# Down-projections: two of four weight sums of a seven-product chunk by transfers, and a third seven-product chunk in the first halves

## The chip, the cores and the metric

The kernel runs on one core of a Trainium2 chip. The metric is device time in microseconds, the median of several runs; lower is better. Engines are named as the profile names them: PE (matrix products) with its weight loads PEld, DVE (VectorE), ACT (ScalarE), POOL (GpSimd), SP (SyncE, which here only issues loads).

## What is computed

Two layers over 256 positions of width 2048, in float32. Each layer is a token mixer and then a gated feed-forward part, and the change lies in the last product of the latter:

```python
def conv_ffn(h, w_up, conv_w, conv_b, w_down):
    u = h @ w_up                          # 2048 -> 11264
    u = conv_width_3(u) + conv_b          # along positions, per channel
    gate, val = jnp.split(u, 2, axis=-1)  # 5632 each
    return (jax.nn.silu(gate) * val) @ w_down   # 5632 -> 2048
...
h = h + conv_ffn(rms_norm(h, ffn_norm[i]), w_up[i], conv_w[i], conv_b[i], w_down[i])
```

## The kernel before

**Tiles.** `w_down` is 11 chunks of 512 rows by four column blocks of 512. A *load* brings half of a chunk's column block, 128 partitions by 1024 numbers, 512 KB, into one of six `raw` buffers (`NRAW`; line 137, issued by SP, which takes its orders one after the other). A float32 factor is split into a high part in float32r and the rest: ACT copies `raw` to `wh` (line 129), DVE subtracts to get `wl` (line 130), and a product is three matmuls, high by high, low by high, high by low. Four pairs `wh`/`wl` go round (`NHL` and one more in the down-projections).

**Stages.** `ffn` works in two halves (`HALVES`), chunks 0 to 5 and 6 to 10. In each half the up-projections make the chunks' activations, and then the down-projection takes the column blocks in pairs, (0,1) and (2,3), each pair by `project_pair`. In layer 0's second half, blocks 2 and 3 are plain projections; in layer 1's second half the pair (2,3) is the `tail`.

**Passes.** `project_pair` goes through a list of passes (`units`), which `weave` writes out. A *column pass* ("c", chunk, i) loads one buffer, splits it and makes 12 matmuls. A *product pass* ("P", chunk, p) is one of the seven products that replace the eight block products of a chunk and a pair of column blocks (Winograd's form); it makes 6 matmuls. So a plain chunk costs a pair 4 x 12 = 48 matmuls, and a seven-product chunk 7 x 6 = 42, with 7 splits in place of 4. `SKG` says which chunks of each half go by seven products: 0 and 2 in both; the tail takes the first alone.

**Weight sums.** The chunk's four weight blocks are "11", "12", "21", "22". Products 1, 2 and 3 take blocks 11, 21 and 22 as loaded, the others take sums, which DVE makes in place in `raw` (line 251) one pass ahead, in `prepare`:

```python
        sums = {5: ("11", "12"), 7: ("12", "22"), 6: ("22", "11"), 4: ("21", "22")}
```

The order of the products is `ORDER` = 1, 2, 5, 3, 7, 6, 4. In a first half each product pass is followed by one column pass while there are any (in pair (0,1) not behind the first product of a chunk, `lone`), after four column passes ahead for the pair (0,1) and one for (2,3).

**Activation sums.** A seven-product chunk needs seven combinations of its activations (`forms`), made and split by `glu_forms` while the next chunk is projected up; a plain chunk needs four splits (`glu`). `make_forms` does the same for chunk 0 of the next up-projection during the first half's down-projection, with its scratch in the tiles "t" and "tT". `combine` adds the products up into `h`.

**Order of the work.** Each engine has one instruction stream, whose order the framework's scheduler sets at build time from the order of the program, with splits and sums moved ahead (`AHEAD`). A `raw` buffer is handed on in the order of release; the next load into it waits until its last reader has finished.

Of the kernel before, what the change touches and what calls it, by code (L numbers as in the profile page):

```python
# [8 lines left out]
F32 = mybir.dt.float32  # L9
# [14 lines left out]
NRAW, NHL = 6, 3  # L24
SKG = ((0, 2), (0, 2))
ORDER = (1, 2, 5, 3, 7, 6, 4)
PLACE = "pava"
AHEAD = 45
# [6 lines left out]
def tile_encoder(ctx: ExitStack, tc: tile.TileContext, x, xT, w_a, w_ao, q_gain, k_gain, w_b, w_bo,  # L35
# [15 lines left out]
    nc.gpsimd.memset(nhalf, -0.5)  # L51
    ones = cpool.tile([P, P], F32, name="ones")
    nc.gpsimd.memset(ones, 1.0)
    nc.scalar.dma_start(gain, gains)
# [6 lines left out]
    def nm(s):  # L61
        uid[0] += 1
        return f"{s}_{uid[0]}"
# [152 lines left out]
    def project_pair(w, n0, n1, lhs, forms, units, late, early_done, n0_done, product_done=None, tail=False,  # L216
                     lazy=False):
        home = {1: "M1", 2: "C11", 3: "C12", 4: "C21", 5: "M5", 6: "M6", 7: "M7"}
# [22 lines left out]
        def block(kg, b):  # L241
            if (kg, b) not in blocks:
                blocks[kg, b] = load_raw(w, (n0, n1)[int(b[1]) - 1], kg, int(b[0]) - 1)
            return blocks[kg, b]

        def prepare(u):
            kind, kg, p = u
            if kind == "P" and p in sums:
                dst, src = (block(kg, b) for b in sums[p])
                with tc.high_priority(offset=AHEAD):  # L250
                    nc.vector.tensor_tensor(dst, dst, src, ALU.add)  # L251
                if p == 6:
                    done_raw(blocks.pop((kg, "11")))
                elif p == 4:
                    done_raw(blocks.pop((kg, "22")))

        last_s = max(i for i, u in enumerate(units) if u[0] == "P")
        for i, (kind, kg, p) in enumerate(units):
# [4 lines left out]
            else:  # L263
                b = {1: "11", 2: "21", 3: "22", 5: "11", 7: "12", 6: "22", 4: "21"}[p]
                r = block(kg, b)
            if i + 1 < len(units):
                prepare(units[i + 1])
            wh, wl = split_raw(r, kind == "c" or p in (7, 4))
            if kind == "P" and p in (7, 4):
                blocks.pop((kg, b))  # L270
# [281 lines left out]
    def ffn(l, hT, ss_in, g_next, last, side=None):  # L552
        with tc.tile_pool(name=nm("wpool"), bufs=1) as wp, tc.tile_pool(name=nm("fpool"), bufs=1) as fp:
# [5 lines left out]
            fin = []  # L559
            cr = fp.tile([P, 3, P], F32, name=nm("cr"))  # L560
            rows = conv[l].rearrange("b o (r c) -> (b o r) c", c=P)
# [13 lines left out]

            us = [fp.tile([P, 1040], F32, name=nm("u"))[:, :1032].rearrange("p (j c) -> p j c", j=4) for _ in range(2)]
            for u in us:
                nc.gpsimd.memset(u[:, :, P:P + 1], 0.0)

# [40 lines left out]
            def form_tiles():  # L620
                xs, ts = (fp.tile([P, 4, NT], F32, tag=t, name=nm("xs")) for t in ("t", "tT"))
                return xs, ts, [fp.tile([P, 2, NT], F32R, tag=t, name=nm("fm"), bufs=3) for t in ("cg", "cg", "cv", "cv")]

            def glu_forms(cg, cv, fm, hh):
# [34 lines left out]
            for hf, (p0, p1) in enumerate(HALVES):  # L659
# [3 lines left out]
                def new_form():  # L663
                    pool, k = next(tags)
                    return tuple(pool.tile([P, NT], F32R, tag=f"a{c}{k}", name=nm("a" + c)) for c in "hl")

                wide.append(1)
                for p in range(p0, p1):
                    if p - p0 in SKG[hf]:
                        fm = forms[p - p0] = {f: new_form() for f in (1, 7, 2, 5, 4, 6, 3) + (0,) * hf}  # L670
                        if hf:
                            for kt in range(4):
                                slots[4 * (p - p0) + kt] = [
                                    tuple(t[:, kt % 2 * P:(kt % 2 + 1) * P] for t in fm[f])
                                    for f in ((1, 0), (2, 4))[kt // 2]]
                    else:
                        slots.update({4 * (p - p0) + j: new_form() for j in range(4)})
# [92 lines left out]
                def weave(lead, late, tail):  # L770
                    ks = SKG[hf][:1] if tail else SKG[hf]
                    c = [("c", k, i) for k in range(np_) if k not in ks for i in range(4)]
                    ps = [("P", k, p) for k in ks for p in ORDER]
                    if tail:
                        c0, c1 = ([u for u in c if u[2] // 2 == n] for n in range(2))
                        c = c0[:-1] + c1[:4] + c0[-1:] + c1[4:-2]
                    units = []
                    units += [c.pop(0) for _ in range(lead)]
                    lone = (ps[0], ps[7]) if late and hf == 0 else ()
                    rest = len(c)  # L780
                    for i, u in enumerate(ps):
                        n = min(1, len(c))
                        if late and hf == 1:
                            n = (i + 1) * rest // len(ps) - i * rest // len(ps)
                        units += [u] + [c.pop(0) for _ in range(n) if u not in lone]
                    return units + c
# [12 lines left out]
                def pair(n0, n1, late, tail=False):  # L799
# [3 lines left out]
                                       lambda a: start(combine(a, n0, n1, fp, "s", combined)),  # L803
                                       lambda a: first_half(a, n0, n1), tail=tail)
                    accs = acc["C12"], acc["C22"]
# [7 lines left out]
                if hf == 0:  # L813
                    start(make_forms(first_forms, hT, 0, form_tiles))
                if hf == 0 or last:
# [564 lines left out]
```

## Time and profile before

| | |
|---|---|
| time, median of 3 runs | 2236.48 us (2235.53 to 2237.12) |
| span of the profiled execution | 2235.3 us; what lies around it is some 1.2 us, taken against the median |
| PE busy | 2222.8 us (99%), 10021 matmuls |
| DVE, ACT, POOL busy | 1838.0 us (82%), 1549.9 us (69%), 329.7 us (15%) |
| granted clock of PE | 0.999 |
| loads of `w_down` | 176 of 512 KB, 4.9 us from issue to landing (median) |
| sums of weight blocks by DVE (line 251) | 92 of 1226 ns; 52 of them in the down-projections |

The profile is one execution. A view of windows gives the busy time of each engine in stretches of time; matmul records overlap (each has some 0.39 us, while the next starts earlier), so PE's busy time says little, and starts and counts say more. "Released by" is what ended an engine's idle time.

### The profile page before, as it was taken

What the parts mean: (1) busy time and instruction counts of PE and PEld (TensorE: products, weight loads), DVE (VectorE), ACT (ScalarE), POOL (GpSimd) and SP (SyncE); (2) the same over time, 40 slices, a digit from 0 to 9 for tenths busy, and PEclk for the clock granted to TensorE, in tenths of its full rate; (3) what the DMA queues carried; (4) which work ended last, traced back from release to release, by engine and by line L of the source; (5) the groups of instructions that cost most, each with busy time, mean ns of one, the idle gap of its engine ahead of it and who ended that gap; (6) DMA issues with size and microseconds to landing.
All of it is one profiled execution on the core that took longest, in us unless ns stands there. A gap on an engine that the chain in (4) does not pass through costs nothing.

```text
span 2235.3 us, 29163 instructions
## 1 busy us (share of the span) xinstructions
PE 2222.8 (99%) x10021; PEld 1840.0 (82%) x10021; DVE 1838.0 (82%) x2523; ACT 1549.9 (69%) x2393; POOL 329.7 (15%) x482
## 2 busy tenths in 40 slices
PE   9999999999999999999999999999999999999998
PEld 7888888888888888888888888888888888888886
DVE  6777778888888788979877978786887898888897
ACT  7665677777557777767876777576777754677764
POOL 2210212210001010011340213010110100001101
PEclk9999999999999999999999999999999999999999
DMA  8444656766556665666655565565566666556654
GB/s 303 164 145 151 206 189 208 243 202 191 199 197 201 200 192 176 225 204 205 212 178 191 166 206 179 188 198 187 193 195 192 197 198 211 190 193 192 227 183 151
DMA packets 126501, 437.44 MB, mean 196 GB/s; under 512 B 17313, under 2 KB 18081, under 8 KB 126353
## 3 DMA queue, kind: packets, MB, share of 16 engines
q1 hardware_dynamic: 119744, 425.64, 58.1%
q0 software_dynamic: 6176, 9.39, 1.7%
q8 instruction: 78, 1.28, 0.2%
q14 instruction: 71, 0.57, 0.1%
q10 hardware_dynamic: 432, 0.56, 0.1%
HBM read 429.20 MB, written 6.29 MB: 195 GB/s over the span
## 4 chain that ended last, share of the span: by engine, by line
PE 93%; DVE 3%; issue 1%; DMA 1%; POOL 1%; ACT 1%; SPq 0%; DVEq 0%; POOLq 0%; ACTq 0%
PE acc L155 18%; PE acc L156 18%; PE acc L154 18%; PE acc L286 11%; PE acc L291 11%; PE acc L288 11%; DVE wl L130 2%; DMA raw<-in_w_down_dram 1%; PE ps L291 1%; PE ps L321 1%; PE ps L286 1%; PE ps L288 1%; PE ps L325 0%; POOL pp L361 0%; PE ps L324 0%
## 5 line engine op out<-in xcount | busy, mean ns | idle before, releaser
L130 DVE TENSOR_TENSOR wl<-raw,wh 128x1024 fp32r<-128x1024 f32 x861 | 1056.8, 1234 | 266.4 <-ACT wh L129 262.3
L129 ACT ACTIVATE wh<-raw 128x1024 fp32r<-128x1024 f32 x861 | 902.6, 1057 | 467.5 <-PE acc L156 166.3
L154 PE MATMUL acc<-wh,xh 128*128 128x512 f32 x1664 | 649.2, 391 | 0.0
L155 PE MATMUL acc<-wl,xh 128*128 128x512 f32 x1664 | 648.8, 390 | 0.3 <-DVE wl L130 0.2
L156 PE MATMUL acc<-wh,xh 128*128 128x512 f32 x1664 | 648.1, 389 | 0.0
L155 PEld LDWEIGHTS acc<-wl,xh 128*128 128x128 f32 x1664 | 312.6, 188 | 67.4 <-DVE wl L130 2.8
L156 PEld LDWEIGHTS acc<-wh,xh 128*128 128x128 f32 x1664 | 312.4, 188 | 64.6
L154 PEld LDWEIGHTS acc<-wh,xh 128*128 128x128 f32 x1664 | 312.7, 188 | 63.7 <-ACT wh L165 0.3
L286 PE MATMUL acc<-wh,ah 128*128 128x512 f32 x762 | 297.0, 390 | 0.6 <-DVE h L544 0.6
L288 PE MATMUL acc<-wh,al 128*128 128x512 f32 x762 | 296.7, 389 | 0.0
L361 POOL COPY u<-t 32x256 f32<-32x256 f32 x176 | 110.5, 628 | 1003.9 <-DVE t L591 995.7
L291 PE MATMUL acc<-wl,ah 128*128 128x512 f32 x762 | 212.0, 389 | 0.4 <-DVE wl L130 0.4
L286 PEld LDWEIGHTS acc<-wh,ah 128*128 128x128 f32 x762 | 143.1, 188 | 31.2 <-DVE h L544 1.5
L291 PEld LDWEIGHTS acc<-wl,ah 128*128 128x128 f32 x762 | 143.0, 188 | 30.4 <-DVE wl L130 0.9
L288 PEld LDWEIGHTS acc<-wh,al 128*128 128x128 f32 x762 | 143.1, 188 | 29.5
L286 PE MATMUL acc<-wh,xh 128*128 128x512 f32 x416 | 162.7, 391 | 0.0
L288 PE MATMUL acc<-wh,xh 128*128 128x512 f32 x416 | 162.0, 389 | 0.0
L363 ACT ACTIVATE u<-t 32x256 f32<-32x256 f32 x352 | 147.6, 419 | 17.8 <-DVE t L591 9.9
L251 DVE TENSOR_TENSOR raw<-raw,raw 128x1024 f32<-128x1024 f32 x92 | 112.8, 1226 | 14.8 <-DMA raw<-in_w_down_dram 14.1
L291 PE MATMUL acc<-wl,xh 128*128 128x512 f32 x416 | 113.1, 390 | 0.0
L288 PEld LDWEIGHTS acc<-wh,xh 128*128 128x128 f32 x416 | 78.1, 188 | 16.0
L286 PEld LDWEIGHTS acc<-wh,xh 128*128 128x128 f32 x416 | 78.1, 188 | 16.0
(254 smaller groups left out, 2388.9 us busy)
## 6 DMA issues: line engine op xcount, KB each, us to landing
raw<-in_w_up_dram SPq DMA_DIRECT2D x352, 512.0 KB, 4.5
raw<-in_w_down_dram SPq DMA_DIRECT2D x176, 512.0 KB, 4.9
raw<-in_w_b_dram SPq DMA_DIRECT2D x144, 512.0 KB, 4.5
raw<-in_w_bo_dram SPq DMA_DIRECT2D x48, 512.0 KB, 4.4
raw<-in_w_a_dram SPq DMA_DIRECT2D x40, 512.0 KB, 4.5
raw<-in_w_ao_dram SPq DMA_DIRECT2D x32, 512.0 KB, 3.8
raw<-in_w_a_dram SPq DMA_DIRECT2D x16, 256.0 KB, 6.1
h<-in_x_dram SPq DMA_DIRECT2D x4, 512.0 KB, 8.4
```

Of the source, the lines that this page charges most:

```text
L129: nc.scalar.activation(wh, r, AF.Copy)
L130: nc.vector.tensor_tensor(wl, r, wh.bitcast(F32), ALU.subtract)
L154: nc.tensor.matmul(accs[m], xh, wh[:, j, :], start=st, stop=False)
L155: nc.tensor.matmul(accs[m], xh, wl[:, j, :], start=False, stop=False)
L156: nc.tensor.matmul(accs[m], xl, wh[:, j, :], start=False, stop=sp)
L251: nc.vector.tensor_tensor(dst, dst, src, ALU.add)
L286: nc.tensor.matmul(acc[k], xh, wh[:, j, :], start=k in fresh, stop=False)
L288: nc.tensor.matmul(acc[k], xl, wh[:, j, :], start=False, stop=False)
L291: nc.tensor.matmul(acc[k], xh, wl[:, j, :], start=False, stop=last[k] == i and j == 1)
L321: nc.tensor.matmul(o, lh[ls], rh[rs], start=start, stop=stop)
L361: nc.gpsimd.tensor_copy(dst, src)
L363: nc.scalar.activation(dst, src, AF.Copy)
```

## The change

Thirteen seven-product chunk passes per execution become seventeen: in both first halves chunk 4 goes by seven products too. In every down-projection two of the four sums of a chunk are made by accumulating transfers that POOL issues: block 22 is added onto 12 from the weights in HBM (a second read of it), and 22, by then 22+11+12, is added onto 21 within the chip's buffers. DVE makes the other two, behind the product whose block they overwrite and no longer one pass ahead. The products' order becomes 1, 2, 3, 5, 6, 7, 4, and blocks 11 and 12 are loaded together. In the first halves the column passes are spread evenly over the 21 product passes (12 column passes: 4 or 1 ahead, 8 or 11 between). The third chunk's activation sums get room in "tT" and "junk", for which `make_forms` moves its scratch to the tiles "u" (whose edges are zeroed again afterwards), the convolution's rows move to "junk", and an unused tile `ones` goes. The products of the attention's and the up-projections' chunks keep the old order and DVE's sums.

```diff
-SKG = ((0, 2), (0, 2))
+SKG = ((0, 2, 4), (0, 2))
 ORDER = (1, 2, 5, 3, 7, 6, 4)
+ORDER_D = (1, 2, 3, 5, 6, 7, 4)
...
+        def onto(kg, b, src):
+            dst = blocks[kg, b].rearrange("p a c -> p (a c)")
+            if isinstance(src, str):
+                src = blocks[kg, src].rearrange("p a c -> p (a c)")
+            nc.gpsimd.dma_start(dst, src, accum_op=ALU.add)
+
+        def add(kg, b, src):
+            with tc.high_priority(offset=AHEAD):
+                nc.vector.tensor_tensor(blocks[kg, b], blocks[kg, b], blocks[kg, src], ALU.add)
+
+        def sums_behind(kg, p):
+            if p == 1:
+                add(kg, "11", "12")
+                if 7 in by_dma:
+                    onto(kg, "12", w[n1, kg][:, 1024:])
+                else:
+                    add(kg, "12", "22")
+            elif p == 3:
+                add(kg, "22", "11")
+                if 4 in by_dma:
+                    onto(kg, "21", "22")
+            elif p == 6 and 4 not in by_dma:
+                add(kg, "21", "22")
+                done_raw(blocks.pop((kg, "22")))
...
-            if i + 1 < len(units):
-                prepare(units[i + 1])
-            wh, wl = split_raw(r, kind == "c" or p in (7, 4))
-            if kind == "P" and p in (7, 4):
+            if by_dma:
+                if kind == "P" and p == 1:
+                    block(kg, "12")
+                if i and units[i - 1][0] == "P":
+                    sums_behind(*units[i - 1][1:])
+                free = (5, 7, 4) + (6,) * (4 in by_dma)
+            else:
+                if i + 1 < len(units):
+                    prepare(units[i + 1])
+                free = (7, 4)
+            wh, wl = split_raw(r, kind == "c" or p in free)
+            if kind == "P" and p in free:
                 blocks.pop((kg, b))
...
-            us = [fp.tile([P, 1040], F32, name=nm("u"))[:, :1032].rearrange("p (j c) -> p j c", j=4) for _ in range(2)]
-            for u in us:
-                nc.gpsimd.memset(u[:, :, P:P + 1], 0.0)
+            ut = [fp.tile([P, 1040], F32, name=nm("u")) for _ in range(2)]
+            us = [t[:, :1032].rearrange("p (j c) -> p j c", j=4) for t in ut]
+            def zero_edges():
+                for u in us:
+                    nc.gpsimd.memset(u[:, :, P:P + 1], 0.0)
...
-                xs, ts = (fp.tile([P, 4, NT], F32, tag=t, name=nm("xs")) for t in ("t", "tT"))
+                xs, ts = (t[:, :1024].rearrange("p (j c) -> p j c", j=4) for t in ut)
...
+            def first_half_forms():
+                yield from make_forms(first_forms, hT, 0, form_tiles)
+                zero_edges()
...
-                        fm = forms[p - p0] = {f: new_form() for f in (1, 7, 2, 5, 4, 6, 3) + (0,) * hf}
+                        fm = forms[p - p0] = {}
+                        if p - p0 == 4:
+                            f2 = fp.tile([P, 4, NT], F32R, tag="tT", name=nm("ff"))
+                            f1 = fp.tile([P, 512], F32R, tag="junk", name=nm("ff"))
+                            fm.update({7: (f2[:, 0], f2[:, 1]), 5: (f2[:, 2], f2[:, 3]), 6: (f1[:, :NT], f1[:, NT:])})
+                        fm.update({f: new_form() for f in (1, 7, 2, 5, 4, 6, 3) + (0,) * hf if f not in fm})
...
-                    ps = [("P", k, p) for k in ks for p in ORDER]
+                    ps = [("P", k, p) for k in ks for p in ORDER_D]
...
-                    lone = (ps[0], ps[7]) if late and hf == 0 else ()
                     rest = len(c)
                     for i, u in enumerate(ps):
                         n = min(1, len(c))
-                        if late and hf == 1:
+                        if hf == 0 or late:
                             n = (i + 1) * rest // len(ps) - i * rest // len(ps)
-                        units += [u] + [c.pop(0) for _ in range(n) if u not in lone]
+                        units += [u] + [c.pop(0) for _ in range(n)]
...
-                                       lambda a: first_half(a, n0, n1), tail=tail)
+                                       lambda a: first_half(a, n0, n1), tail=tail, by_dma=(7, 4))
```

More of the change, by code (lines that the diff above doesn't have):

```diff
@@ L51, in tile_encoder @@
     nc.gpsimd.memset(nhalf, -0.5)
-    ones = cpool.tile([P, P], F32, name="ones")
-    nc.gpsimd.memset(ones, 1.0)
     nc.scalar.dma_start(gain, gains)
@@ L216, in project_pair @@
     def project_pair(w, n0, n1, lhs, forms, units, late, early_done, n0_done, product_done=None, tail=False,
-                     lazy=False):
+                     lazy=False, by_dma=()):
         home = {1: "M1", 2: "C11", 3: "C12", 4: "C21", 5: "M5", 6: "M6", 7: "M7"}
@@ L559, in ffn @@
             fin = []
-            cr = fp.tile([P, 3, P], F32, name=nm("cr"))
+            cr = fp.tile([P, 512], F32, tag="junk", name=nm("cr"))[:, :3 * P].rearrange("p (a c) -> p a c", a=3)
             rows = conv[l].rearrange("b o (r c) -> (b o r) c", c=P)
@@ L620, in form_tiles @@
             def form_tiles():
-                xs, ts = (fp.tile([P, 4, NT], F32, tag=t, name=nm("xs")) for t in ("t", "tT"))
+                xs, ts = (t[:, :1024].rearrange("p (j c) -> p j c", j=4) for t in ut)
                 return xs, ts, [fp.tile([P, 2, NT], F32R, tag=t, name=nm("fm"), bufs=3) for t in ("cg", "cg", "cv", "cv")]
+            def first_half_forms():
+                yield from make_forms(first_forms, hT, 0, form_tiles)
+                zero_edges()
             def glu_forms(cg, cv, fm, hh):
@@ L813, in ffn @@
                 if hf == 0:
-                    start(make_forms(first_forms, hT, 0, form_tiles))
+                    start(first_half_forms())
                 if hf == 0 or last:
```

## The prediction

> **What bounds the kernel now.** I read the page's busy times first, then the down-projections' stretches in the view of windows, then the timeline for the beat of PE, and last the waits of SP and ACT there and the DMA issues.
>
> ```profile
> span 2235.3 us, 29163 instructions
> ...
> PE 2222.8 (99%) x10021; PEld 1840.0 (82%) x10021; DVE 1838.0 (82%) x2523; ACT 1549.9 (69%) x2393; POOL 329.7 (15%) x482
> ...
> 526.00:651.70 125.70, 125.12 (x552) 103.26 (x551) 112.97 (x129) 70.90 (x84) 2.58 (x4) 1.00 0.60 200
> 526.00:588.60 62.60, 62.60 (x278) 51.82 (x277) 58.13 (x74) 40.78 (x54) 2.58 (x4) 1.00 0.58 192
> 869.00:920.50 51.50, 51.50 (x229) 42.62 (x228) 50.11 (x59) 35.41 (x48) 2.58 (x4) 1.00 0.57 191
> 1778.50:1904.00 125.50, 125.43 (x553) 103.54 (x552) 113.19 (x129) 71.32 (x84) 2.59 (x4) 1.00 0.61 201
> 2172.70:2221.00 48.30, 47.85 (x211) 39.33 (x210) 43.89 (x46) 23.64 (x31) 8.43 (x5) 1.00 0.47 161
> ...
> 565.46 0.39 PE L286 MATMUL acc<-wh,ah 128*128 128x512 f32 x1
> 565.69 0.39 PE L288 MATMUL acc<-wh,al 128*128 128x512 f32 x1
> 565.91 0.39 PE L286 MATMUL acc<-wh,ah 128*128 128x512 f32 x1
> ```
>
> The rows of windows are: stretch, its length, then PE, PEld, DVE, ACT and POOL busy with counts, PE's clock, DMA share, GB/s. They are, in order, layer 0's first half (both pairs), its pair (0,1), layer 0's second-half pair, layer 1's first half, and the tail. A matmul has 0.39 us, but the next starts 0.227 us after it; so 0.227 and not 0.39 is what a matmul costs, a product pass is 6 x 0.227 = 1.36 us and a column pass 2.72. The 552 matmuls of a first half's two pairs take 552 x 0.2267 = 125.1 us of the 125.7 in the first of these rows: PE stands idle for 0.6 us in layer 0, 0.4 in layer 1, 0.5 in the tail (211 x 0.2267 = 47.8 of 48.3), nothing in the second-half pair. PE bounds these stages, and DVE is close behind, 58.1 of 62.6 us in the pair (0,1).
>
> How far the splits run ahead of PE, S below, decides what a late buffer costs:
>
> ```profile
> 520.70 1.22 DVE L130 TENSOR_TENSOR wl<-raw,wh 128x1024 fp32r<-128x1024 f32 x1
> 526.02 0.39 PE L286 MATMUL acc<-wh,ah 128*128 128x512 f32 x1
> 563.90 1.22 DVE L130 TENSOR_TENSOR wl<-raw,wh 128x1024 fp32r<-128x1024 f32 x1
> 567.27 1.07 PE L291 MATMUL acc<-wl,ah 128*128 128x512 f32 x4
> ...
> ACT wh L129 <- PE acc L288: 24.7, 21, 5.1
> ACT wh L129 <- DMA raw<-in_w_down_dram: 12.1, 7, 2.8
> ...
> SPq L137 <- DVE wl L130: 85.8, 39, 7.5
> ```
>
> Counting splits and passes in order, these are the first and the twentieth of the stretch 526 to 588.6: the first column pass needs its low part 8 matmuls after 526.02, at 527.83, and has it at 521.9, S = 5.9; the twentieth needs it at 567.27 and has it at 565.1, S = 2.2. I take S = 3. The waits (total, times, longest; 526 to 651.7) say what limits S: mostly ACT waits until PE gives back a pair, which is idle time with no price; 12.1 us it waits for loads; and SP stands 85.8 of 125.7 us before a raw buffer is free. Loads go out as fast as buffers come back.
>
> **The change part by part.**
>
> *Matmuls.* Chunk 4 costs a pair 42 in place of 48, over two pairs and two layers 24 fewer: 24 x 0.2267 = 5.44 us off the engine that bounds the stage. This is the gain.
>
> *Splits and DVE's sums.* Their prices, and the stage that makes the third chunk's activation sums:
>
> ```profile
> L130 DVE TENSOR_TENSOR wl<-raw,wh 128x1024 fp32r<-128x1024 f32 x59 | 70.9, 1220 | 7.4 <-ACT wh L129 7.0
> L251 DVE TENSOR_TENSOR raw<-raw,raw 128x1024 f32<-128x1024 f32 x17 | 20.8, 1221 | 4.8 <-DMA raw<-in_w_down_dram 4.7
> L129 ACT ACTIVATE wh<-raw 128x1024 fp32r<-128x1024 f32 x60 | 62.1, 1057 | 50.6 <-PE acc L288 24.7 <-DMA raw<-in_w_down_dram 12.1 <-DVE raw L251 8.8
> L307 DVE TENSOR_TENSOR fm<-xs,fm 128x256 fp32r<-128x256 f32 x4 | 1.7, 417 | 0.0
> ...
> 460.00:510.00 50.00, 50.00 (x222) 41.38 (x222) 39.87 (x58) 37.48 (x58) 7.46 (x12) 1.00 0.64 209
> ```
>
> In a first-half pair passes go from 30 to 33 and DVE's sums from 8 to 6: DVE has one operation more, 58.13 + 1.22 = 59.35 us, in 62.6 - 1.36 = 61.2 us; ACT has 40.8 + 3 x 1.06 = 44.0. Hidden behind PE, with 1.9 us to spare on DVE where there were 4.5. Without this cover the 1.22 us is paid in each of four pairs, 4.9 us. In the second-half pairs DVE loses 4 sums of 8 (4.9 us of 50.1) and in the tail 2 of 4; PE has nothing to regain in the former and at most 0.5 us in the latter. Over all, at most 0.6 + 0.4 + 0.5 = 1.5 us of stall can be regained. I take the tail's alone, as DVE is what is relieved there: 0.5.
>
> *The third chunk's activation sums.* Seven splits for four and four more small sums: 7 x 0.42 = 2.9 us for DVE and 3 x 0.41 = 1.2 for ACT, once a layer, while chunk 5 is projected up. There DVE has 39.9 us in 50 (last row): hidden, and 2.9 us a layer if it were not. The two small memsets of edges and the moved scratch are order on POOL and DVE, at nothing; behind a memset that waits for the sums' last split, POOL's next transfer would wait too.
>
> *The order on SP.* The same 24 loads a pair; block 12 comes 1 to 3 passes sooner, so it holds its buffer longer, block 11 shorter (given back at product 5). Evenly spread, the column passes give the products less cover: between two product passes 8/21 of a column pass and not nearly one.
>
> *The transfers.* Two of 512 KB a chunk, 34 in all, from POOL, which waits for DVE's sum before it issues; behind it stand only the last up-projection's four copies, the edges, and in the tail the final gains, none of which PE waits for soon. The trace has no accumulating transfer. The nearest rows, of windows about 2101, 1055, 367, 1130 and, for the loads beside nothing else, 526 to 588.6:
>
> ```profile
> q1 hardware_dynamic: 3291, 11.99, 57.9%
> raw<-in_w_down_dram SPq DMA_DIRECT2D x23, 512.0 KB, 4.9
> DMA to landing us min/median/max: 3.7/4.9/6.9
> ...
> btg<-scr POOLq DMA_DIRECT2D x1, 256.0 KB, 5.6
> fin<-in_final_norm_dram POOLq DMA_DIRECT2D x4, 256.0 KB, 5.1
> scr<-lnt POOLq DMA_DIRECT2D x6, 256.0 KB, 12.5
> ...
> raw<-in_w_b_dram SPq DMA_DIRECT2D x4, 512.0 KB, 4.3
> raw<-in_w_down_dram SPq DMA_DIRECT2D x5, 512.0 KB, 5.9
> raw<-in_w_b_dram SPq DMA_DIRECT2D x4, 512.0 KB, 7.4
> bt<-scr POOLq DMA_DIRECT2D x3, 256.0 KB, 7.2
> ```
>
> From below it is the fastest load, 3.7 us; from above, POOL's transfers out in small pieces, 12.5. Between: 57.9% of 62.6 us for 11.99 MB is 3.0 us of all 16 engines per MB, so 1.6 us for 512 KB, and a load's other 3.3 us (4.9 - 1.6) is fixed. POOL's lone 256 KB took 5.6, where SP's price would be 3.3 + 0.8 = 4.1: 1.5 us for the way through POOL. An add reads its destination too, so I count its 512 KB twice, 3.2. Together 3.3 + 1.5 + 3.2 = 8.0 us: L = 8, nearer to the loads than to the small pieces, since its rows are the loads' rows of 4 KB.
>
> The Trainium skill ("DMA: Bandwidth & Descriptors", section "Anatomy of one DMA — SWDGE (gpsimd) path") fits such a transfer by 2.0 us plus the bytes at 436 GB/s, which would be an estimated 3.2 us for 512 KB; by it no transfer would be late and the time 2230.6 us. The trace's 5.6 us for half the bytes disagrees.
>
> What L costs: block 21's sum follows the split of product 3 and must land before product 4's split. From the first split's end: 1.2 us DVE's sum, L, 1.06 + 1.22 the last split; PE meanwhile has S, 1.36 of product 3's span, and the passes between. So it is late by L + 2.1 - S - gap. The gap is 3 product passes and two column passes, 4.1 + 5.4 = 9.5 us, nearly everywhere; it has one column pass, 6.8 us, for chunks 2 and 4 of each first half's pair (0,1), and four in the tail. With S = 3 the limits are 7.7 and 10.4. Block 12's sum has 8.2 to 10.9 us and stands better. A third limit: block 22's buffer is held until the transfer has read it, and the next load in it, in chunk 0 of pair (0,1) wanted 14.5 us after product 3, has 14.5 + 3 - 1.2 - 4.9 - 2.3 = 9.1 us. At L = 8 four chunks are late by 0.3 us each, 1.2 in all.
>
> **Sum.** -5.44 + 1.2 - 0.5 = -4.7 us. The profiled execution's 2235.3 us of span becomes 2230.6; against the median, 1.2 us above that span, 2236.5 - 4.7 = 2231.8. What can be told from no change is 0.2%, 4.5 us.
>
> **The rivals.**
>
> *The sums land late (slower).* The place is product 4 of chunks 2 and 4 of pair (0,1), the price 1 us of PE for each us of L above 7.7, four times. At L = 9.1 the gain is spent, at 10.2 it is 0.2% slower: 4 x 2.5 - 5.4 = 4.6. At 12.5, 4 x 4.8 = 19.2, and the twelve other chunks with a gap of 9.5 add 12 x 2.1 = 25: 2236.5 - 5.4 + 44 = 2275. For it: the 12.5 row and the unknown rate of an add. Against: the small pieces of that row.
>
> *The loads land late.* Two transfers beside 6.7 loads a chunk. The DMA's 0.58 in the window becomes (24 x 1.6 + 6 x 3.2) / 61.2 = 0.94. Where POOL's and SP's transfers met, a load took 7.4 us and not 4.9. A chunk of 16.8 us with six buffers has 101 us of buffer time; the holds that I add up from the passes (load, 2.3 us of split, passes between) are 14, 17, 19 and 16 us for the four blocks and 2.7 x 7.2 for column passes, 85 in all, so 16 us are to spare, 2.4 a load. A load of 7.4 takes 6.7 x 2.5 = 16.8; with L 1.5 us longer too, 2.3 us are missing, over six buffers 0.4 us for each of 12 first-half chunks: 2236.5 - 5.4 + 4.8 = 2236. The same page of the Trainium skill ("Queues, rings and completion order") states the rule: each engine takes the queues in turn, packet by packet. The trace agrees by the 7.4. Against it: beside btg's 5.6 and fin's 5.1 the loads took 4.3 and 5.9.
>
> *DVE becomes the bound.* It has 59.35 of 61.2 us; if the idle 4.5 us it had in that pair cannot be used, it needs 63.8 and PE loses 2.6 us in each layer's pair (0,1): 2236.5 - 5.4 + 5.2 = 2236. For it: S shrinks to 2.2 where DVE has the last chunk's activations to finish. Against: most of that idle time was PE's back-pressure.
>
> **How the numbers follow.** Forecast (hidden but for small rests, 2229.6 to 2232): 0.44. Late loads 0.20 and DVE 0.12, both about 2236, within 0.2%. Late sums, 2241 to 2275: 0.24. So faster 0.44, same 0.32, slower 0.24. The range goes from all stalls regained and none new, 2236.5 - 5.4 - 1.5 = 2229.6, up to L = 11, where 4 x 3.3 + 12 x 0.6 - 5.4 = 15 us are lost, 2251; the likeliest case's own is 2229.6 to 2233.
>
> **What would show it.** 9997 matmuls; 873 splits; 74 sums on line 251's successors; PE idle under 1 us in each first-half stage, now about 122.5 to 123.5 us long. L in the DMA issues: up to 8 right, above 9 wrong. Waits of ACT for accumulating transfers, ended late enough that PE waits for wh or wl, are the first rival; landings of `w_down` above 6.5 us the second; DVE busy above 98% of the pair (0,1) with PE waiting for wl the third. The forecast is wrong if an add moves its bytes much slower than a load.

## The result, and the profile after

The changed kernel takes 2258.1 us (median of 4 runs, 2257.06 to 2258.94) against 2236.8 us beside it: a ratio of 1.0096, with a 95% interval of 1.0084 to 1.0108. It is slower by 21 us, where 2231.8 us were forecast and the range ended at 2251.0. Line numbers below are those of the changed kernel: PE's products are L318, L320, L323, ACT's splits L128, DVE's L129, its two sums L253, POOL's transfers L249, the additions of a finished pair into `h` L576.

The page's head:

```profile
span 2255.3 us, 29294 instructions
...
PE 2223.1 (99%) x9997; PEld 1834.6 (81%) x9997; DVE 1835.9 (81%) x2531; ACT 1562.6 (69%) x2411; POOL 360.7 (16%) x519
```

The view of windows (columns as before: stretch, length, the engines' busy time and counts, PE's clock, DMA share, GB/s) for layer 0's first half (two pairs), its second-half pair, and layer 1's first half:

```profile
526.70:660.20 133.50, 124.97 (x540) 100.46 (x539) 110.45 (x122) 75.98 (x90) 13.32 (x18) 1.00 0.80 225
866.00:918.00 52.00, 52.00 (x231) 43.07 (x230) 44.11 (x57) 38.36 (x55) 5.18 (x7) 1.00 0.73 213
1790.50:1923.00 132.50, 126.22 (x543) 102.16 (x542) 111.34 (x123) 76.56 (x90) 13.25 (x18) 0.99 0.81 230
```

The 24 matmuls are gone (9997), and the second-half pair, transfers and all, still has a PE that never stands idle. Most of the loss is in the first halves: 540 matmuls should take 540 x 0.2267 = 122.4 us and take 133.5, so 11.1 us are lost there, and some 10 in layer 1, where PE's clock has a part in it (0.99; see the last section). A few more are lost at the entry to the up-projection behind.

The waits of the whole run (total, times, longest):

```profile
PE acc L318 <- ACT wh L128: 9.6, 7, 3.2
PE acc L318 <- DVE h L576: 6.2, 4, 2.5
PE ps L318 <- DVE cu L569: 2.6, 1, 2.6
...
ACT wh L128 <- DMA raw<-raw: 54.5, 15, 6.3
ACT wh L128 <- DMA raw<-in_w_down_dram: 37.7, 34, 4.3
```

In the kernel before, PE had one wait for an addition:

```profile
PE acc L286 <- DVE h L544: 0.6, 1, 0.6
```

The issues of transfers (size of one, median from issue to landing):

```profile
raw<-in_w_down_dram SPq DMA_DIRECT2D x176, 512.0 KB, 5.1
raw<-in_w_down_dram POOLq DMA_DIRECT2D x17, 512.0 KB, 5.9
raw<-raw POOLq DMA_DIRECT2D x17, 512.0 KB, 6.8
```

PE now waits in two ways. It waits 9.6 us for a high part `wh`, which in five of the seven cases (7.7 us) ACT couldn't make because the transfer `raw<-raw` (block 22's sum onto 21, product 4's weights) hadn't landed. And it waits 8.8 us (6.2 and 2.6) at the ends of pairs for DVE's additions. Yet a transfer lands after 6.8 us by the median, sooner than the 8 that I counted. The timeline of the largest stall, chunk 2's product 4 in pair (0,1), engine by engine, shows how:

```profile
555.79 2.36 DVE L129 TENSOR_TENSOR wl<-raw,wh 128x1024 fp32r<-128x1024 f32 x2
558.07 1.22 DVE L253 TENSOR_TENSOR raw<-raw,raw 128x1024 f32<-128x1024 f32 x1
559.82 0.86 POOL L249 DMA_DIRECT2D raw<-raw  x1 [5.31 <-DVE raw L253]
568.42 1.06 ACT L128 ACTIVATE wh<-raw 128x1024 fp32r<-128x1024 f32 x1 [6.27 <-DMA raw<-raw]
569.51 1.23 DVE L129 TENSOR_TENSOR wl<-raw,wh 128x1024 fp32r<-128x1024 f32 x1 [5.47 <-ACT wh L128]
565.69 0.61 PE L323 MATMUL acc<-wl,ah 128*128 128x512 f32 x2
569.53 0.50 PE L318 MATMUL acc<-wh,ah 128*128 128x512 f32 x1 [3.23 <-ACT wh L128]
```

The splits of products 3 and 5 are the two at 555.79; product 3's is done at 556.97, but its sum starts only behind the other, at 558.07. POOL issues 0.5 us after the sum, and ACT starts on the data 8.6 us after that. ACT has been idle for 6.3 us and DVE for 5.5: both take their orders in turn, so no later split could be made meanwhile, though the load for the next one (issued at 554.29, 6.7 us) had landed by 561. Behind the stall the splits have no lead left.

### The profile page after: what moved, and what is told of

Its sections match the earlier page's. It is cut to its first block, busy times and chain, and to the rows that moved or that the text cites. A ratio compares the mean times of both kernels' runs of the same rounds, so it can differ in the third digit from the quotient of the medians.

```text
span 2255.3 us, 29294 instructions
## 1 busy us (share of the span) xinstructions
PE 2223.1 (99%) x9997; PEld 1834.6 (81%) x9997; DVE 1835.9 (81%) x2531; ACT 1562.6 (69%) x2411; POOL 360.7 (16%) x519
## 5 line engine op out<-in xcount | busy, mean ns | idle before, releaser
L129 DVE TENSOR_TENSOR wl<-raw,wh 128x1024 fp32r<-128x1024 f32 x873 | 1068.7, 1233 | 296.7 <-ACT wh L128 290.9
L128 ACT ACTIVATE wh<-raw 128x1024 fp32r<-128x1024 f32 x873 | 914.4, 1056 | 478.0 <-PE acc L155 158.8
L154 PEld LDWEIGHTS acc<-wl,xh 128*128 128x128 f32 x1664 | 312.5, 188 | 68.5 <-DVE wl L165 2.8
L318 PE MATMUL acc<-wh,ah 128*128 128x512 f32 x730 | 286.2, 392 | 14.5 <-ACT wh L128 9.6
L320 PE MATMUL acc<-wh,al 128*128 128x512 f32 x730 | 285.1, 391 | 0.0
L323 PE MATMUL acc<-wl,ah 128*128 128x512 f32 x730 | 205.8, 391 | 0.3
L318 PEld LDWEIGHTS acc<-wh,ah 128*128 128x128 f32 x730 | 137.6, 189 | 46.9 <-ACT wh L128 12.5
L318 PE MATMUL acc<-wh,xh 128*128 128x512 f32 x416 | 162.9, 392 | 1.2 <-DVE h L576 1.2
L320 PE MATMUL acc<-wh,xh 128*128 128x512 f32 x416 | 162.0, 389 | 0.0
L323 PEld LDWEIGHTS acc<-wl,ah 128*128 128x128 f32 x730 | 136.6, 188 | 31.0 <-DVE wl L129 3.0
L320 PEld LDWEIGHTS acc<-wh,al 128*128 128x128 f32 x730 | 137.5, 188 | 28.3
L323 PE MATMUL acc<-wl,xh 128*128 128x512 f32 x416 | 113.2, 390 | 0.2 <-DVE wl L129 0.2
L318 PEld LDWEIGHTS acc<-wh,xh 128*128 128x128 f32 x416 | 78.1, 188 | 18.1 <-DVE h L576 2.1
L323 PEld LDWEIGHTS acc<-wl,xh 128*128 128x128 f32 x416 | 77.9, 188 | 16.8 <-DVE wl L129 0.6
L320 PEld LDWEIGHTS acc<-wh,xh 128*128 128x128 f32 x416 | 78.1, 188 | 16.0
```

Of the source, the lines that this page charges most:

```text
L128: nc.scalar.activation(wh, r, AF.Copy)
L129: nc.vector.tensor_tensor(wl, r, wh.bitcast(F32), ALU.subtract)
L154: nc.tensor.matmul(accs[m], xh, wl[:, j, :], start=False, stop=False)
L318: nc.tensor.matmul(acc[k], xh, wh[:, j, :], start=k in fresh, stop=False)
L320: nc.tensor.matmul(acc[k], xl, wh[:, j, :], start=False, stop=False)
L323: nc.tensor.matmul(acc[k], xh, wl[:, j, :], start=False, stop=last[k] == i and j == 1)
```

## The experiments

Each edit is against the changed kernel unless it says otherwise. The letters of theories in the expectations are those of the text in which they stand.

| run | median us | ratio to before, 95% interval |
|---|---|---|
| e1 two chunks | 2236.7 | 1.0001 (0.9991 to 1.0010) |
| e2 fourth sum by DVE | 2235.1 | 0.9994 (0.9985 to 1.0004) |
| e3 two column passes between | 2253.7 | 1.0078 (1.0063 to 1.0093) |
| e4 all of the chunk's sums by DVE | 2248.0 | 1.0055 (1.0040 to 1.0070) |
| e5 two between, one last | 2243.9 | 1.0033 (1.0020 to 1.0046) |
| e6 a quarter of the fourth transfer | 2245.1 | 1.0041 (1.0026 to 1.0056) |
| e7 seventh sum by DVE | 2276.6 | 1.0177 (1.0160 to 1.0194) |
| e8 fourth by DVE in pairs (0,1) | 2247.3 | 1.0050 (1.0035 to 1.0065) |
| e9 fifth sum left out | 2261.4 | 1.0112 (1.0098 to 1.0126) |
| e10 two between, two or three last | 2245.2 | 1.0041 (1.0027 to 1.0055) |
| e11: e2, three column passes last | 2236.0 | 1.0000 (0.9991 to 1.0009) |
| e12: e2, two last | 2236.1 | 0.9999 (0.9990 to 1.0008) |
| e13 seventh buffer | 2258.9 | 1.0098 (1.0084 to 1.0112) |
| e14: e2 and a seventh buffer | 2232.7 | 0.9983 (0.9974 to 0.9992) |
| e15: e5 and a seventh buffer | 2240.6 | 1.0018 (1.0009 to 1.0027) |
| e16: e10 and a seventh buffer | 2243.5 | 1.0032 (1.0020 to 1.0044) |
| e17 fourth transfer from the weights | 2233.4 | 0.9990 (0.9980 to 0.9999) |
| e18: e17 and a seventh buffer | 2238.5 | 1.0008 (0.9998 to 1.0017) |

**Transfers without the third chunk.**

```diff
-SKG = ((0, 2, 4), (0, 2))
+SKG = ((0, 2), (0, 2))
```

> The changed kernel with the first halves' seven-product chunks back at 0 and 2; transfers, order and even spread stay. Theory A (product 4's sum lands late where few column passes lie between products 3 and 4, and the splits queued behind it leave DVE idle, whose debts fall due at the pair's end): with 12 or 15 column passes over 14 product passes there are at least 4.1 + 2 x 2.7 = 9.5 us between, mostly 12, so no stall at all, 2236 us, within 3 us of before. Theory B (DVE, at 97% in the pair (0,1), is the bound): DVE has 4 sums fewer a pair than before, so also 2235 to 2237. Theory C (any accumulating transfer costs PE, whatever the spacing): 14 transfers fewer than 34, of each first-half pair 4 remain, so about two thirds of the loss, 2250.

2236.7 us: 26 transfers, the new order and the even spread cost nothing with two chunks, though the transfers land no sooner:

```profile
raw<-in_w_down_dram POOLq DMA_DIRECT2D x13, 512.0 KB, 6.7
raw<-raw POOLq DMA_DIRECT2D x13, 512.0 KB, 6.6
```

**Which transfer.** e2 is `by_dma=(7,)`; e4 is `by_dma=()` with `ORDER` in place of `ORDER_D`; e7 is `by_dma=(4,)` with block 22 loaded behind product 1.

> The changed kernel with product 4's sum made by DVE behind product 6 (17 operations of 1.22 us more), product 7's sum still by transfer. Theory A: the waits for the buffer-to-buffer transfer go (54.5 us of ACT's waits), and DVE pays 3 x 1.22 = 3.7 us more a first-half pair; in the pair (0,1) that is 63 us of work in 61.2, so 2 to 4 us are lost per layer: 2238 to 2243. Theory B: DVE being the bound already, 3.7 us more in each of four pairs comes on top: 2265 or more.

> The third chunk alone: all four sums by DVE one pass ahead, in the old order, the column passes spread evenly as in the changed kernel; no transfers. DVE has 3 splits and 4 sums more than before in each first-half pair, 58.1 + 8.5 = 66.7 us of work in 61.2 in the pair (0,1) and 63.3 in the pair (2,3). Theory A: DVE is the bound here and only here, 5.5 + 2 us lost per layer, 15 in all, less 5.4: 2246. If the transfers are what the changed kernel loses its time to, this is faster than it; Theory B: DVE's work decides, this has 6 operations a pair more than the changed kernel, so 2270 or more.

> The changed kernel with product 7's sum made by DVE behind product 1, so that block 22 is loaded with 11 and 12, and product 4's sum still by transfer. Theory A: product 4's lateness stays and DVE has 3.7 us more a first-half pair, so slower than the changed kernel: 2262 to 2275. If the second read of block 22 from HBM (17 transfers beside the loads) is what costs, this is faster than the changed kernel: 2245 or less.

With product 4's sum by DVE the loss is gone, 2235.1 us, although DVE then does one operation more a chunk and product 7's transfers remain. Without any transfer the third chunk costs 11 us, and with product 4's alone 40. ACT's wait for DVE's sums in e4:

```profile
ACT wh L128 <- DVE raw L275: 56.7, 39, 3.5
```

and PE's for high parts in e7, 15.7 us where the changed kernel had 9.6 (L319 there is L318 here):

```profile
PE acc L319 <- ACT wh L128: 15.7, 12, 3.6
```

So product 4's transfer is the one that costs, and it costs more with one more DVE sum behind product 1 and block 22 loaded sooner (e7). What product 7's transfer alone is worth isn't separated: e4, whose ACT waits 56.7 us for DVE's sums one pass ahead, also has the old order of the products.

**How much of it, and where.** e6 moves only the first 256 of 1024 columns by product 4's transfer; e8 is `by_dma=(7,) if hf == 0 and late else (7, 4)`; e9 leaves away `add(kg, "11", "12")`.

> The changed kernel with the transfer for product 4's sum cut to a quarter, 128 partitions by 256 numbers (three quarters of that sum are left out). Orders, waits, DVE's and PE's work stay; only the landing comes sooner, some 4 to 4.5 us from issue in place of 6.8. Theory A: product 4 is then late by less than 1.5 us anywhere and most stalls go, those at the pairs' ends too, since they are DVE's debts from its waits: 2233 to 2240. Theory D: the ends keep their 10 us, the insides lose their 13: 2243 to 2248. Theory F (the wait goes through POOL's issue and the order of the queues, and not the moving of bytes): 2252 or more.

> Product 4's sum by DVE only in the first halves' pairs (0,1), six sums in all; the other eleven by transfer. As predicted, the four chunks with a gap of 6.8 us would be the only late ones, and this would bring the time to 2232 to 2236. Theory A as it now stands (splits run only 1 to 2 us ahead when DVE is full, so a gap of 9.5 us is too short too): the pairs (2,3) stay late by 1 to 2 us twice a layer and their ends too, some 4 us a layer: 2238 to 2244.

> The changed kernel without DVE's sum for product 5 (block 11 goes in alone, so the output is short of that part; the sums for 6 and 4 lack it too): one DVE operation of 1.22 us fewer per seven-product chunk, transfers, matmuls and splits as they are. If how far the splits run ahead is what decides (DVE 97% busy, splits 2 us ahead in place of the 3 that were reckoned with), DVE gains 1.2 us a chunk, product 4 of chunk 2 is late by 1 to 2 us in place of 3.9, and the ends, where DVE comes 1 to 3 us earlier, lose half: 2240 to 2247. If the landing alone decides, 2255 or more.

The issues of e6:

```profile
raw<-raw POOLq DMA_DIRECT2D x17, 128.0 KB, 5.3
```

and its timeline at the first stall, ACT's split of product 4 and PE's first matmul of it:

```profile
565.73 1.06 ACT L128 ACTIVATE wh<-raw 128x1024 fp32r<-128x1024 f32 x1 [4.21 <-DMA raw<-raw]
566.84 0.50 PE L318 MATMUL acc<-wh,ah 128*128 128x512 f32 x1 [0.55 <-ACT wh L128]
```

e6's transfer lands sooner by about 2 us at the same place, PE's first stall falls from 3.2 us to 0.55, and 12 us of 21 come back. In e8 the pairs (2,3), where I had counted a gap of 9.5 us, are late too, and 11 us remain: the gap of pair (0,1) isn't the whole. e9 takes 17 sums off DVE and is no faster (2261.4), so less work for DVE isn't enough. It is no clean test of DVE's load, though: PE's longest wait for `wh` falls to 1.1 us, but product 7's transfers now take 8.0 us by the median in place of 5.9, and ACT waits for these (4.0 us at 575.84).

**The ends of pairs.** PE needs an accumulator that DVE must first add into `h`. In e3 no column pass stands behind a pair's last product; e5 leaves one, e10 two or three, all with two or three between products 3 and 4 of each chunk:

```diff
-                        if hf == 0 or late:
+                        if hf == 0:   # e5; e3 has i < 14 in place of i == 6
+                            n = ((0, 0, 1, 0, 0, 1, i == 6) if late else (0, 0, 1, 0, 1, 1, i == 6))[i % 7]
+                        elif late:
```

> The changed kernel with the same passes in another spread in the first halves: in every seven-product chunk of the pair (0,1) two column passes, and of the pair (2,3) three, lie between products 3 and 4, where the changed kernel has one or two. No engine has an operation more or less. Theory A: product 4's sum has 9.5 and 12.3 us in place of 6.8 and 9.5, more than landing (6.8 us in the middle) and splits need, so most of the 23 us of stall goes: 2232 to 2240. Theory B: DVE's work is the same, 2255 to 2260. Theory D (the stalls at the pairs' ends, some 8 us, have a cause of their own): only the waits inside the pairs go, 2243 to 2247.

> The changed kernel with two column passes (pair (0,1)) or three (pair (2,3)) between products 3 and 4 of each first-half chunk, as in the run with two between, but one column pass kept behind the last product of the pair. In the run with two between, no wait for a transfer inside a pair cost PE more than 1.2 us, and 15.1 us went to DVE's additions into h at the pairs' ends, where nothing was left to do behind product 4. Theory A (lateness inside, debts at the end): with the last column pass as cover, both go; 24 matmuls less count: 2231 to 2237. Theory D (the ends stall by themselves, since DVE is full): the ends keep the changed kernel's 10 us: 2240 to 2245.

> All sums as in the changed kernel. As in the run with two column passes between products 3 and 4 and one last, but two (pair (0,1)) or three (pair (2,3)) column passes behind the pair's last product, taken from behind product 4 of chunk 0 and from chunk 4. In that run the four ends still cost 2.0 us each, since DVE has four splits and three or four small operations in line between the split of the last product and the addition into h that frees the bank, 6 to 7.6 us, and PE has 4 us of passes left. With 2.7 to 5.4 us more of cover the ends should go: 2244 - 7 = 2237, 2234 to 2239. If the ends are due to DVE's load alone, no change: 2242 or more.

PE's waits for the additions in e3:

```profile
PE acc L318 <- DVE h L576: 15.1, 4, 5.3
```

in e5, with that for splits:

```profile
PE acc L318 <- DVE h L576: 7.2, 4, 2.0
...
PE acc L318 <- ACT wh L128: 0.2, 1, 0.2
```

and in e10, where none for additions is left:

```profile
PE acc L318 <- ACT wh L128: 3.4, 7, 0.9
PE acc L323 <- DVE wl L129: 2.5, 4, 1.1
```

The timeline of the changed kernel at the end of layer 0's pair (0,1), from the splits of the last product (by ACT, then DVE) to the addition and the matmul that waits for it:

```profile
587.48 2.96 ACT L128 ACTIVATE wh<-raw 128x1024 fp32r<-128x1024 f32 x3 [3.93 <-DMA raw<-raw]
588.57 1.22 DVE L129 TENSOR_TENSOR wl<-raw,wh 128x1024 fp32r<-128x1024 f32 x1 [2.90 <-ACT wh L128]
...
595.52 0.68 DVE L576 TENSOR_TENSOR h<-acc,h 128x512 f32<-128x512 f32 x1
596.26 0.50 PE L318 MATMUL acc<-wh,ah 128*128 128x512 f32 x1 [2.44 <-DVE h L576]
```

ACT had waited 3.9 us for the transfer of the pair's last chunk, and DVE 2.9 us for ACT, so this end begins with a late transfer too. From 588.57 to 596.2 DVE has 7.6 us of splits and small sums in a row. PE has less than that to do behind the last product, unless column passes stand there: 15.1, 7.2 and no such wait with none, one, and two or three. With two or three passes always between products 3 and 4, e5 waits 0.2 us in all for `wh`: a wide enough gap takes the stalls inside the pairs away. e10 has clean ends, and waits 5.9 us for splits between them instead. Moving passes shifts the loss, and takes back two thirds of it at most (e5, 13 us of 21).

e11 and e12 put the last column passes of e2 in the same way, `rest - 2` or `rest - 1` in the spread:

> Product 4's sum by DVE (as in the run that took 2235.1), and three column passes in place of one behind the last product of each first-half pair, the others spread evenly before. In that run PE's only long stall in the first halves is 3.9 us at the end of layer 0's, where DVE is late with combining the products. With 5.4 us more of cover it goes: 2231 to 2232.5. If DVE's load decides, the passes taken away earlier let PE run into DVE there instead: 2235 to 2239.

> The same with two column passes behind the last product: half the cover, 2.7 us more than in the run that took 2235.1; 2231 to 2233 if cover at the end is what it lacked, 2235 to 2237 if DVE's load is.

Neither differs from e2.

**Buffers.** A seventh raw buffer in a tile that is free in the first halves' down-projections (the list of buffers gets it behind the first pair's sixth pass, and loses it after the second pair).

> The changed kernel with one raw buffer more (seven) in the first halves' down-projections, in a tile that is free there; nothing else differs. Theory A (the loss is a matter of buffers: each transfer holds two raw buffers for its 6 to 8.5 us, so the next loads go out late, the splits lose their lead of 2 to 3 us and don't rebuild it, and every wait after that is paid by PE): a seventh buffer adds 17% of buffer time, the lead comes back, SP's wait for a free buffer and ACT's 37.7 us of waits for loads shrink by a third or more, the rests inside the pairs go (some 13 us of 25) and the pair ends shrink; 2236 to 2245 us. Theory B (transfer too long for the gap between products 3 and 4, whatever the lead): the first rest stays at 3 to 4 us and the time at 2253 to 2258. Theory C (DVE too full to keep a lead): no change, 2256 to 2259.

> Product 4's sum by DVE (product 7's by a transfer, three chunks by seven products), and a seventh raw buffer in the first halves' down-projections. With six buffers this gave 2235.1, within the noise of the kernel before, although it has 24 matmuls fewer (5.4 us). Theory A (buffers): the remaining rests, some 5 us more than in the kernel before, go, and the time is 2231 to 2234. Theory C (DVE too full): 2235 to 2236.

> The changed kernel with one column pass left behind the last product of a pair and the others moved between products (2243.9 with six buffers, of which some 7 us were the four pair ends), and a seventh raw buffer. Theory A: the lead at the pair ends grows from under 2 to above 3 us, the rests there go, 2234 to 2239. Theory C: 2243 to 2245.

> The changed kernel with two (pair (0,1)) and three (pair (2,3)) column passes behind the last product (2245.2 with six buffers; pair ends clean, inside the pairs 0.4 to 1.2 us at each of many places, ACT waiting for loads 62.8 us), and a seventh raw buffer. Theory A: the waits for loads shrink by half, 2233 to 2239. Theory C: 2244 to 2246.

The theory I held was that the transfers' hold on buffers makes the loads late and so eats the lead. A seventh buffer doesn't bear it out: e13 is as slow as the changed kernel. The same stall in it, with ACT's wait and PE's (its lines stand two to four further down):

```profile
569.78 1.06 ACT L130 ACTIVATE wh<-raw 128x1024 fp32r<-128x1024 f32 x1 [6.80 <-DMA raw<-raw]
570.89 0.80 PE L322 MATMUL acc<-wh,ah 128*128 128x512 f32 x1 [5.04 <-ACT wh L130]
```

The transfer, issued at 560.24, takes 9.5 us in place of 8.6. The loads beside it go out no sooner (559.68 and 560.77, where they went at 559.35 and 560.45), so why it takes longer stays open. Measured against the kernel before beside each, the buffer is worth 2.0 us with product 4's sum by DVE (e14 and e2), and with the wider gap 3.6 (e15 and e5) and 1.4 (e16 and e10, within the noise): it helps where the chain isn't what binds. e14's 2232.7 us is faster than both kernels, by 0.17% of the kernel before. In its first half DVE is busy for 118.37 us of 122.50, and PE hardly stands:

```profile
526.00:648.50 122.50, 122.19 (x537) 100.11 (x536) 118.37 (x131) 77.01 (x89) 8.06 (x12) 1.00 0.78 232
```

**The chain.** Product 4's transfer adds block 22 from the weights, behind product 2; it waits for no sum. It leaves 11+12 out of product 4's weights, so e17 and e18 tell of times and are not kernels to use:

```diff
             elif p == 3:
                 add(kg, "22", "11")
-                if 4 in by_dma:
-                    onto(kg, "21", "22")
+            elif p == 2 and 4 in by_dma:
+                onto(kg, "21", w[n1, kg][:, 1024:])
```

> The changed kernel, but product 4's transfer adds block 22 onto 21 from the weights in HBM, issued behind product 2, and not the sum 22+11+12 behind product 3: it waits for no sum by VectorE. It leaves the part 11+12 out of product 4's weights. Number, size and bytes of the transfers stay as they are, and so does VectorE's work. Theory B (the chain behind product 3, that is a split, the sum of 1.2 us, the hand-over and 8.5 to 9.5 us of transfer, is longer than the gap to product 4): the transfer starts some 3.8 us sooner (a sum, a split and a pass of 1.36), so the stalls of 3.6 and 2.6 us at product 4 of chunk 2 go, as do the smaller ones at chunk 4, and the pair ends (2 to 2.6 us each) stay or shrink: 2240 to 2248 us. Theory D (two transfers beside the loads are more than the DMA engines bear in this stretch, wherever they wait): 2252 to 2259 us, with ACT waiting for loads of weights instead.

> The same (the part 11+12 left out of product 4's weights) with a seventh raw buffer in the first halves' down-projections. With the long chain a seventh buffer gave nothing (2258.9 us), with one transfer a chunk it gave 2.4 us. Theory B: with the chain short the loads profit from the buffer, the lead at the pair ends grows above 2.4 us and two or more of the four ends become clean: 2234 to 2242 us. Theory D: as without it, 2250 to 2259 us.

2233.4 us: with as many transfers of the same size and DVE's work as in the changed kernel, some 24 us come back, more than I expected, since the ends of pairs went too. The issues of e17:

```profile
raw<-in_w_down_dram POOLq DMA_DIRECT2D x34, 512.0 KB, 7.2
```

its timeline at the same place, POOL's issue and ACT's split of product 4:

```profile
554.56 0.86 POOL L249 DMA_DIRECT2D raw<-in_w_down_dram  x1 [1.18 <-DVE wl L129]
562.52 1.06 ACT L128 ACTIVATE wh<-raw 128x1024 fp32r<-128x1024 f32 x1 [1.49 <-DMA raw<-in_w_down_dram]
```

its first half in the view of windows:

```profile
526.00:649.80 123.80, 122.50 (x540) 100.98 (x539) 112.68 (x125) 77.59 (x90) 13.32 (x18) 1.00 0.86 253
```

and PE's waits at the ends of pairs:

```profile
PE acc L318 <- DVE h L576: 2.5, 2, 1.3
```

The transfers land no sooner (7.2 us; product 4's own 8.2 by the median, where it was 6.8), and the DMA engines are busier than in the changed kernel (0.86, where it was 0.80). But this one leaves at 554.56 and not at 559.82, and the split follows at 562.52 and not at 568.42, in time. 540 matmuls take 123.8 us. That shows the cause: product 4's weights wait on a chain of split, split, DVE's sum, hand-over and transfer that is longer than the gap, and the stall of the in-order engines behind it sets off the rest; the traffic and DVE's load, which stayed, don't. One thing came along: this transfer doesn't read block 22's buffer, so SP's waits for `raw<-raw` (78.1 us, 15 times in the changed kernel) are gone too. e13 says that a buffer alone is worth nothing there, but SP waits for that transfer as long in it (35.4 us in layer 0's first half, 33.3 in the changed kernel). A chain cut with that hold left in wasn't tried, so how much of the 24 us is the hold stays open. The extra buffer of e18 made it 5 us slower, against my expectation; the last section has about half of why.

## Why the prediction was wrong

*The gain.* Right: 24 matmuls fewer, 873 splits, 34 sums at L253 and 40 at its sister line (74). e17 at 3.1 us below its kernel before and e14 at 3.4 are near the forecast's 4.7, once product 4's weights are in time. The second-half pair stayed at no stall; the tail's 0.5 us came, since PE's one wait in it, 0.45 us at 2191.4 in the kernel before, is gone.

*The transfer.* L was taken as 8.0 us and has a median of 5.9 and 6.8, so "up to 8 right" was met, and still the sums landed late. What I asked of the profile was the wrong number: not the median but the landing at the tight place decides, 8.6 us there. The Trainium skill's fit ("DMA: Bandwidth & Descriptors", "Anatomy of one DMA — SWDGE (gpsimd) path") would be an estimated 3.2 us; the trace's 5.9 and 6.8 disagree.

*The lateness: the step that failed.* "Late by L + 2.1 - S - gap" named the right place and mechanism, but S = 3 and the chain's length were mis-sized. Counted back from 565.69, product 4 was wanted at 566.15; 6.8 + 1.36 us earlier, at 557.98, stands product 3, whose low part is wanted at 558.89 and was done at 556.97: S = 1.9. DVE takes a further split of 1.2 before the sum, and the hand-over to POOL is 0.5. So 8.6 + 0.5 + 1.2 + 2.1 - 1.9 - 6.8 = 3.7 us, where the forecast had 0.3; measured are 3.4 us, and 0.2 more at the low part. The same working for the first chunk of pair (2,3), with its gap of 9.5 us, gives 8.7 + 0.5 + 1.2 + 2.1 - 1.3 - 9.5 = 1.7 us late, where the forecast had nothing; measured are 1.3, at 616.31.

*That the stalls stand alone.* I added up late chunks as if each began again with a lead of 3 us. It isn't rebuilt: between that stall and the end of the pair there is little slack, pairs (2,3) with the wider gap are late as well (e8), and pairs end in waits for DVE's additions, 8.8 us in the waits. No term of the sum had the ends. That they are mostly the same loss, passed on, is what e17 shows: 2.5 us remain there.

*The rivals.* "The sums land late" (0.24) was the right one; its price as written at L = 6.8 would have been nothing. "Loads land late": loads took 5.1 us, and a seventh buffer changed nothing in the changed kernel; not the cause, though worth 2 us beside e2. "DVE becomes the bound": e2 and e14 speak against it, which give DVE one more sum a chunk; in e14 it is busy for 118.4 of 122.5 us, and PE hardly stands.

## What to carry to other kernels

A transfer that replaces an engine's operation is to be judged by the whole chain that it stands in, from the last reader of its destination to the first user of its result, with the landing at its tightest place and the lead measured there. Where engines take their orders in turn, one late operand stops all that follow and uses up the lead for the rest of the stage. A source that needs no other engine's result was worth more here than moved passes or a buffer, but e17 leaves a part of the weights out to have it; to start the transfer a pass earlier wasn't tried. What gained time and leaves nothing out is DVE's own sum for product 4, with a seventh buffer (e14).

## What the runs showed of the hardware

**A short stall can halve PE's clock.** In e13, behind the stall of 5.04 us, the windows from 570.8 on have a granted clock of 0.50 (the column before the last two):

```profile
570.80:573.00 2.20, 2.11 (x5) 1.73 (x6) 2.13 (x4) 1.83 (x5) 0.11 (x1) 0.50 0.89 244
573.00:576.00 3.00, 3.00 (x8) 2.32 (x8) 2.97 (x4) 2.72 (x3) 0.10 (x1) 0.50 0.95 351
```

In e18 it fell behind a stall of 1.96 us at the end of pair (0,1); the timeline of PE:

```profile
590.11 0.50 PE L322 MATMUL acc<-wh,ah 128*128 128x512 f32 x1 [1.96 <-DVE h L580]
591.24 0.63 PE L324 MATMUL acc<-wh,al 128*128 128x512 f32 x1
591.67 0.63 PE L322 MATMUL acc<-wh,ah 128*128 128x512 f32 x1
```

and the window behind it:

```profile
591.00:593.50 2.50, 2.50 (x8) 1.93 (x7) 2.50 (x5) 0.74 (x1) 1.49 (x2) 0.50 0.06 21
```

A matmul then starts every 0.43 us in place of 0.227, for 12 in e13 and 7 in e18, so the stall costs 2.4 and 1.4 us more than itself. In e18 this happens at both pairs (0,1): 2.8 of the 5.2 us by which its span is longer than e17's. The stall of 3.2 us at 569.53 in the changed kernel was followed by matmuls at the full rate. In its layer 1, a stall of 2.47 us before 1833.18 was followed by half the clock, and one of 2.48 us before 1860.28 was not:

```profile
1835.00:1837.00 2.00, 2.00 (x6) 1.63 (x5) 2.00 (x4) 2.00 (x3) 0.11 (x1) 0.50 1.03 416
1860.30:1862.00 1.70, 1.70 (x7) 1.40 (x8) 1.70 (x2) 0.86 (x2) 0.11 (x1) 1.00 0.79 323
```

So the length alone doesn't decide. The Trainium skill ("TensorE: Matmul & The Clock Gate", "What's actually happening") has the clock halved after an idle window of some 3.4 us, on windows that run freely, and full again after about as long a busy one. The half rate and its length agree (0.50, some 3 to 6 us), and free windows would let the same stall end either way; but a fall after 1.96 us of idleness is shorter than the page's idle window.

**An accumulating transfer** of 512 KB landed after 5.9 us (from HBM) and 6.8 (within the chip) by the median, and 7.2 where two a chunk come from HBM. At the tight place 8.6 us (9.5 in e13) passed from its issue to the split behind it; a quarter of the bytes still took 5.3 by the median.
